# A planned two-layer trunk: copies exchanged for transfers, and the order planned anew with another account of the DMA engines

## The chip, the core and the metric

The kernel runs on one core of one Trainium2 chip. A core has five engines, each with its own in-order queue: TensorE (PE, with its weight loads as PEld), VectorE (DVE), ScalarE (ACT), GpSimd (POOL) and SyncE (SP), which here only issues transfers. An instruction waits on semaphores for what it needs, and everything behind it on its engine waits with it. The metric is the device time of one execution in microseconds, the median of several runs.

## The reference

Two layers are computed on x, 512 rows by 1024 columns, float32. Each layer is

```python
h = x @ w_in                          # 512x2048, cut into q, k, v, u (512 columns each)
A = diff_attention(q, k, v)           # 4 heads; rotary; two causal softmaxes, p0 - lam*p1; RMSNorm
B = s5_ssm(u)                         # 32 groups, complex diagonal scan over 512 steps; GELU; GLU
x = layer_norm(ALPHA*x + concat(A, B) @ w_out)
x = layer_norm(ALPHA*x + relu(x @ w_ff1)**2 @ w_ff2)      # inner width 4096
```

All of it has to hold to float32 accuracy. So each large product is made of three: both operands are split into a high part (a cast to the matmul type) and the remainder.

## The kernel before, in words

**Recording and planning.** The code in `trunk` doesn't issue instructions. It records them (`Rec.add`), with their tiles and dependences. `Rec.cost` gives each a duration, and for a transfer a time on the shared DMA engines (`op.move`) and a fixed part (`op.fix`). `Rec.run` then builds a list schedule by these numbers: each engine takes the ready instruction of the highest priority, which is the longest path behind it plus offsets from the table `PLAN` ("pri" by group of instructions, "fine" by single instruction, "ao", "so", "ap", "sp", "po" by kind). `issue` emits everything in the planned order. So an engine's order is decided by the table and the cost numbers together, before anything runs. Where the planner sees PE idle it may put products of a zero tile into the gap (`wz`, "fillers"); they do no useful work.

**Weights.** `wsplit` (and `gsplit` for the second feed-forward product) loads a block of 128 x 1024 into a `raw` buffer, casts it on ACT into `whi`, and makes the remainder `wlo` in one of three ways, chosen by letters in the table: "V" subtracts on DVE, "P" subtracts on POOL, "A" writes the negated block with ACT and lets POOL issue a DMA that adds the block in flight. There are five `raw` and four `whi`/`wlo` buffers. "lo" holds the letters of the input products, "flo" those of w_ff1, "glo" and "elo" those of w_ff2, "nlo" those of w_out. `mm3` makes the three matmuls of one product: high by high, and each high by the other's remainder.

**A layer.** The front part computes the blocks of "back" (u, q, k, v by number) on PE, and between them attention heads (`attn_u`, one per head and row block; `attn_fin` per head) and the four quarters of the S5 part (`ssm_pars` or `ssm_load`, `ssm_outp`, `ssm_a`, `ssm_b`, `ssm_c`). In layer 1 the first four blocks are multiplied by halves of the rows, since the rows of x come out of the layer norm before. Then come w_out with a layer norm, and eight steps of the feed-forward part, in which seven products replace eight ("m1" to "m7", with sums of weight blocks and of hidden blocks made on DVE), and the last step with the second layer norm.

**Copies and transfers.** Four places can move data within on-chip memory by ACT copies ("A") or by DMA ("D"), per layer: "um" rearranges u in `uproj` (D: one ACT copy into `rt`, a write to DRAM tile `ud`, four reads back), "qm" spreads q and k over partition halves in `qkproj` (D: one ACT cast and one DVE subtraction of the whole tile, then four transfers for q or eight for k; A: casts and subtractions by halves, and for k two memsets), and "mm" fills the block-Toeplitz matrix `mx` in `ssm_outp` (A: six ACT copies of 32 partitions and one of 128 per quarter; D: three transfers and the one copy). `start` loads the first two weight blocks and the eight slices of x in the order written, with "cuts" as the borders of the parts in which the weight blocks come.

**Names and lines.** In the trace all instructions that the planner issues stand at one line, L534, so tiles tell them apart: `whi`, `wlo` and `raw` are weights, `xTh` and `xTl` the split activations, `slot` and `xq` work tiles, `at` attention tiles, `mh` and `y` hold hidden activations of the feed-forward part and the halves of the mix, and `ps_acc`, `ps_sc` and `ps_s` the PSUM banks. "q1"-like names in the table are blocks. The planner's transfer times are at lines 296 to 298 and 485 to 487, `vproj` is at 1072, `attn_u` at 1110.

## Time and profile before

| | us |
|---|---|
| median of 3 runs (lowest, highest) | 1128.52 (1127.23, 1130.73) |
| profiled execution, its own time | 1130.64 |
| its span, first to last instruction | 1128.9 |
| PE busy | 1101.6 |
| DVE busy | 919.5 |
| ACT busy | 609.3 |
| POOL busy | 199.0 |

The profiled execution took 1130.64 us, of which 1.7 us lie outside the span. Times of single instructions are those of this execution. Matmul records overlap, as PE starts one before the other has left the array, so a stretch that is wholly busy can still be slowed by the clock or by small products. The column PEclk tells the granted clock: 1.00 is 2.4 GHz, 0.50 is 1.2 GHz.

### The profile page before, as it was taken

The page shows a single profiled execution, that of the slowest core. Times are in us where ns is not written, and L with a number is a line of the kernel's source. Part 1 is how long each engine was busy: PE and PEld are TensorE (multiplying, and loading weights), DVE is VectorE, ACT ScalarE, POOL GpSimd, SP SyncE. Part 2 cuts the span into 40 slices and gives each one's busy share as a digit, 9 for nine tenths or more (in the row PEclk, how much of TensorE's full clock was granted, in tenths as well). Part 3 has the DMA queues.
Part 4 walks back from the last instruction along what each step waited for, and adds up shares of the span by engine and source line. Part 5 has one row for each costly group of instructions (what it writes and reads, how often), then busy time and mean ns, then how long its engine had stood idle before and what let it go on. Part 6 is the DMA issues. An engine that isn't in the chain of part 4 may idle for free.

```text
span 1128.9 us, 15944 instructions
## 1 busy us (share of the span) xinstructions
PE 1101.6 (98%) x5738; PEld 929.7 (82%) x5738; DVE 919.5 (81%) x1575; ACT 609.3 (54%) x1060; POOL 199.0 (18%) x180
## 2 busy tenths in 40 slices
PE   9999989999999999999998999999999999999996
PEld 6889867898888888888788878888988888888885
DVE  7999998888778877877973789857778779778877
ACT  6557878246454464455343767952455445454440
POOL 1112111121211211211021221113112103103101
PEclk9999989999999999999999999999999999999999
DMA  9755645334555455465788764652444554565341
GB/s 312 193 138 109 161 124 155 116 112 115 147 159 131 122 164 134 119 178 148 224 226 208 179 163 106 194 145 81 141 131 131 149 149 119 144 159 148 105 130 74
DMA packets 59582, 167.73 MB, mean 149 GB/s; under 512 B 7408, under 2 KB 11888, under 8 KB 59504
## 3 DMA queue, kind: packets, MB, share of 16 engines
q1 hardware_dynamic: 48848, 127.92, 35.6%
q0 software_dynamic: 10656, 38.80, 18.6%
q8 instruction: 45, 0.74, 0.3%
q14 instruction: 33, 0.27, 0.1%
HBM read 112.17 MB, written 9.44 MB: 108 GB/s over the span
## 4 chain that ended last, share of the span: by engine, by line
PE 85%; DVE 6%; DMA 6%; ACT 3%; issue 1%; SPq 0%; POOL 0%; DVEq 0%; POOLq 0%; ACTq 0%
PE ps_acc L534 45%; PE ps_sc L534 28%; PE ps_s L534 12%; DVE slot L534 2%; DMA wlo<-raw 2%; DVE xq L534 1%; DMA rt<-rt 1%; DVE rt L534 1%; DMA raw<-in_w_v_dram 1%; DMA raw<-in_w_u_dram 1%; DMA keep<-xq 1%; DMA xq<-rt 1%; ACT at L534 0%; DMA slot<-in_xt_dram 0%; ACT whi L534 0%
## 5 line engine op out<-in xcount | busy, mean ns | idle before, releaser
L534 ACT CAST whi<-raw 128x1024 fp32r<-128x1024 f32 x222 | 233.3, 1051 | 284.2 <-PE ps_acc L534 177.9
L534 PE MATMUL ps_acc<-xTh,wlo 128*128 128x512 f32 (+1 forms) x712 | 268.5, 378 | 3.0 <-DMA wlo<-raw 1.9
L534 PE MATMUL ps_acc<-xTh,whi 128*128 128x512 f32 (+1 forms) x712 | 269.9, 380 | 0.7 <-ACT xTh L534 0.6
L534 PE MATMUL ps_acc<-xTl,whi 128*128 128x512 f32 (+1 forms) x712 | 268.7, 379 | 0.5 <-DVE xTl L534 0.5
L534 PE MATMUL ps_sc<-whi,slot 128*128 128x512 f32 x784 | 251.4, 390 | 1.3 <-DVE xq L534 1.3
L534 DVE TENSOR_TENSOR wlo<-raw,whi 128x1024 fp32r<-128x1024 f32 x114 | 139.0, 1226 | 56.6 <-ACT whi L534 56.6
L534 PEld LDWEIGHTS ps_sc<-whi,slot 128*128 128x128 f32 x784 | 147.1, 188 | 32.6 <-DVE xq L534 1.3
L534 POOL DMA_DIRECT2D wlo<-raw x74 | 65.0, 879 | 523.1 <-ACT rt L534 168.6
L534 PEld LDWEIGHTS ps_acc<-xTh,wlo 128*128 128x128 f32 x712 | 134.1, 188 | 26.7 <-DMA wlo<-raw 3.4
L534 PEld LDWEIGHTS ps_acc<-xTh,whi 128*128 128x128 f32 x712 | 134.0, 188 | 25.4 <-ACT xTh L534 1.8
L534 PEld LDWEIGHTS ps_acc<-xTl,whi 128*128 128x128 f32 x712 | 134.2, 188 | 24.2 <-DVE xTl L534 1.9
L534 PE MATMUL ps_sc<-wlo,slot 128*128 128x512 f32 x392 | 152.7, 390 | 0.0
L534 DVE TENSOR_TENSOR slot<-slot 128x512 fp32r<-128x512 f32 (+4 forms) x143 | 105.9, 755 | 7.8 <-ACT slot L534 7.0
L534 POOL TENSOR_TENSOR wlo<-raw,whi 128x1024 fp32r<-128x1024 f32 x34 | 85.0, 2501 | 151.5 <-ACT whi L534 124.2
L534 DVE TENSOR_TENSOR xq<-xq,ps_sc 128x512 f32<-128x512 f32 x124 | 83.6, 681 | 25.8 <-PE ps_sc L534 25.8
L534 ACT ACTIVATE wlo<-raw 128x1024 fp32r<-128x1024 f32 x74 | 78.3, 1060 | 29.0 <-PE ps_acc L534 18.5
L534 PEld LDWEIGHTS ps_sc<-wlo,slot 128*128 128x128 f32 x392 | 73.6, 188 | 15.2
L534 DVE TENSOR_TENSOR raw<-raw 128x1024 f32<-128x1024 f32 x56 | 68.2, 1218 | 14.2 <-DMA raw<-in_w_ff_dram 13.5
L534 ACT CAST slot<-slot 128x512 fp32r<-128x512 f32 x56 | 34.6, 618 | 50.9 <-DVE slot L534 48.4
L534 PE MATMUL ps_acc<-wlo,xTh 128*128 128x256 f32 (+1 forms) x176 | 55.6, 322 | 3.1 <-DMA wlo<-raw 3.1
L534 PE MATMUL ps_acc<-whi,xTh 128*128 128x256 f32 (+1 forms) x176 | 56.3, 324 | 0.2 <-ACT rt L534 0.2
L534 PE MATMUL ps_acc<-whi,xTl 128*128 128x256 f32 (+1 forms) x176 | 55.9, 321 | 0.0
(228 smaller groups left out, 1846.1 us busy)
## 6 DMA issues: line engine op xcount, KB each, us to landing
raw<-in_w_ff_dram SPq DMA_DIRECT2D x128, 512.0 KB, 3.6
wlo<-raw POOLq DMA_DIRECT2D x74, 512.0 KB, 5.3
raw<-in_w_qk_dram SPq DMA_DIRECT2D x16, 512.0 KB, 5.0
raw<-in_w_out_dram SPq DMA_DIRECT2D x16, 512.0 KB, 3.6
raw<-in_w_u_dram SPq DMA_DIRECT2D x8, 512.0 KB, 4.8
raw<-in_w_v_dram SPq DMA_DIRECT2D x8, 512.0 KB, 7.0
rt<-rt SPq DMA_DIRECT2D x64, 64.0 KB, 2.8
at<-in_ln_dram SPq DMA_DIRECT2D x16, 256.0 KB, 3.9
```

Source lines behind the costliest of these rows:

```text
L534: getattr(self.real[op.eng], op.name)(*[_real(x) for x in op.a], **{n: _real(x) for n, x in op.k.items()})
```

## The change

Four switches change sides. u of layer 1 goes from transfers to copies (u of layer 0 stays with transfers); q of layer 0 goes to copies and k of layer 0 to transfers; q of layer 1 goes to transfers; the Toeplitz blocks of both layers go to transfers. The first two weight blocks come in two parts of 256 and 768 columns. The first two row blocks of each head, not only the first, have both score maps in one bank, which takes one mask product and one maximum instead of two. The planner's account of a transfer is another: other rates and fixed parts, and a transfer that runs beside one of the other queue now slows that one too. The offsets ("pri", 130 groups; "fine"), the places of heads and S5 quarters, two lists of blocks and the letters of the remainders are all other ones. `vproj` has a second layout of its weights under the switch "vw", which is off in both layers.

```diff
-        "q0 u0 k0 u1 v0 u2 v1 q1 k1 u3 q2 v2 k2 v3 q3 k3 g0 g1 g2 g3".split(),
-        "u0 k0 u2 q0 u1 v0 v1 q1 k1 u3 v2 q2 k2 v3 q3 k3 g0 g1 g2 g3".split(),
+        "u0 q0 k0 u1 v0 u2 v1 q1 k1 u3 q2 v2 k2 v3 q3 k3 g0 g1 g2 g3".split(),
+        "u0 k0 u1 u2 q0 v0 v1 q1 k1 u3 v2 q2 k2 v3 q3 k3 g0 g1 g2 g3".split(),
     ],
-    "att": [[8, 11, 15, 19], [8, 12, 15, 18]],
-    "s5": [[1, 13], [10, 14]],
+    "att": [[8, 12, 14, 22], [9, 10, 15, 18]],
+    "s5": [[4, 14], [6, 14]],
...
-    "lo": ["AAAVAAPAAAAVAAAAAAAA", "AAAAAAAAAAAAAPAVAAVP"],
...
-    "flo": "VPVV",
-    "nlo": "APVAVPVA",
-    "glo": "APVVAAV",
+    "lo": ["AAAVPAPAAAAVAAAAAAAP", "AAAAAAAAAAAAAAAVAAVA"],
...
+    "flo": "AVPP",
+    "nlo": "APVAVPPV",
+    "glo": "AVPPAPV",
...
-    "elo": "VVVV",
+    "elo": "AVPV",
...
-    "cuts": [0, 8],
+    "cuts": [0, 2, 8],
...
-    "um": ["D", "D"],
-    "qm": ["DA", "AA"],
-    "mm": ["A", "A"],
+    "um": ["D", "A"],
+    "qm": ["AD", "DA"],
+    "mm": ["D", "D"],
...
-    "one": 1,
+    "one": 2,
...
-            op.move = rows * runs / 16 * (47.0 + o.idx.size * 4 / runs / 35.0) * (2.0 if e != "DMA" else 1.0)
-            op.fix = 50.0 if e != "DMA" or not on[0] else 990.0 if on[1] else 890.0
-            return (660.0 if rows < 128 else 500.0) if e == "DMA" else 1030.0, 1000.0 + op.fix + 1.3 * op.move
+            op.move = rows * runs / 16 * (33.0 + o.idx.size * 4 / runs / 32.1) * (1.7 if e != "DMA" else 1.0)
+            op.fix = 30.0 if e != "DMA" or not on[0] else 750.0 if on[1] else 586.0
+            return (660.0 if rows < 128 else 500.0) if e == "DMA" else 1030.0, 1463.0 + op.fix + 1.3 * op.move
...
-                q, z = ("POOL", "DMA") if e == "POOL" else ("DMA", "POOL")
-                b = max(move[q], op.t1 + 1000.0)
-                move[q] = b + op.move + min(op.move, max(0.0, move[z] - b))
+                q, z, r, u = ("POOL", "DMA", 0.515, 0.734) if e == "POOL" else ("DMA", "POOL", 0.266, 0.485)
+                b = max(move[q], op.t1 + 1463.0)
+                both = max(0.0, min(op.move / r, move[z] - b))
+                move[q] = b + op.move + both * (1 - r)
+                move[z] += both * u
```

How the order moves is seen at three places. The first is ACT near the end of layer 0's attention. Before, between a head's output (`jk`, `at<-ps_sc`) and the first exponentials of the next head (`at,smx<-ps_sc,nm`), ACT has this:

```order
L534 COPY at_1660<-ps_sc_1821 128x128
L534 CAST xq_1933<-rt_1783 64x512 x2
L534 ACTIVATE slot_1366<-slot_1366 128x512
L534 ACTIVATE at_1660<-at_1660,f4_1947 128x128 x4
L534 COPY mx0_108<-m3_1774 32x128 x3
L534 ACTIVATE mh_1974<-ps_sc_1954,sm_115 128x512
L534 COPY mx0_108<-m3_1774 32x128 x3
L534 COPY mx0_108<-m3_1774 128x128
L534 ACTIVATE y_1987<-ps_s5_1963 128x512
L534 ACTIVATE u_764<-ps_s5_1963 128x512
L534 CAST xq_1998<-rt_1783 64x512 x2
L534 ACTIVATE at_2011,smx_2012<-ps_sc_1907,nm_2003 128x128
```

Now, from the last Toeplitz copy of one quarter to the exponentials of the next head:

```order
L538 COPY mx0_98<-m3_1601 128x128
L538 ACTIVATE slot_1266<-slot_1266 128x512
L538 CAST xq_1753<-rt_1161 64x512
L538 CAST xq_1760<-rt_1161 64x512
L538 ACTIVATE y_1779<-ps_s5_1768 128x512
L538 ACTIVATE u_629<-ps_s5_1768 128x512
L538 ACTIVATE at_1822,smx_1823<-ps_sc_1790,nm_1814 128x128
L538 ACTIVATE at_1826,smx_1823<-ps_sc_1790,nm_1814 128x128
L538 COPY mx0_98<-m3_1642 128x128
```

The six 32-partition copies of `mx` have left ACT for SP's queue, and of the four half-tile casts of k two of q are left.

The second place is PE at the v blocks of layer 1: `ps_acc_6096` before and `ps_acc_6059` now are v0, `whi` and `wlo` its weights in two blocks. Before:

```order
L534 MATMUL ps_acc_6096<-whi_5988,xTh_141 128x256
L534 MATMUL ps_acc_6096<-wlo_6002,xTh_141 128x256
L534 MATMUL ps_acc_6096<-whi_5988,xTl_157 128x256
L534 MATMUL ps_acc_6096<-whi_6023,xTh_141 128x256
L534 MATMUL ps_acc_6096<-wlo_6012,xTh_141 128x256
L534 MATMUL ps_acc_6096<-whi_6023,xTl_157 128x256
L534 MATMUL ps_acc_6096<-whi_6023,xTh_141 128x256
```

Now, where `ps_acc_6091` is v1:

```order
L538 MATMUL ps_acc_6059<-whi_5952,xTh_131 128x256
L538 MATMUL ps_acc_6059<-wlo_5962,xTh_131 128x256
L538 MATMUL ps_acc_6059<-whi_5952,xTl_141 128x256
L538 MATMUL ps_acc_6059<-whi_5983,xTh_131 128x256
L538 MATMUL ps_acc_6059<-wlo_5972,xTh_131 128x256
L538 MATMUL ps_acc_6091<-whi_5952,xTh_131 128x256
L538 MATMUL ps_acc_6091<-wlo_5962,xTh_131 128x256
L538 MATMUL ps_acc_6091<-whi_5952,xTl_141 128x256
```

Before, v0 runs from the first weight block straight through the second. Now two products of the second block stand in v0, and PE goes on with v1 on the first block. The blocks ahead of v are u0, k0, u2, q0 and u1 before, and u0, k0, u1, u2 and q0 now.

The third is POOL in layer 0's feed-forward part, where `wlo<-raw` is the issue of an adding DMA and `wlo<-raw,whi` a subtraction on POOL. Before:

```order
L534 DMA wlo<-raw 128x1024 x3
L534 TENSOR_TENSOR wlo<-raw,whi 128x1024 x2
L534 DMA wlo<-raw 128x1024
L534 TENSOR_TENSOR wlo<-raw,whi 128x1024
L534 DMA wlo<-raw 128x1024 x2
L534 TENSOR_TENSOR wlo<-raw,whi 128x1024
L534 DMA wlo<-raw 128x1024 x3
L534 TENSOR_TENSOR wlo<-raw,whi 128x1024 x2
L534 DMA wlo<-raw 128x1024
L534 TENSOR_TENSOR wlo<-raw,whi 128x1024
```

Now:

```order
L538 DMA wlo<-raw 128x1024 x3
L538 TENSOR_TENSOR wlo<-raw,whi 128x1024 x2
L538 DMA wlo<-raw 128x1024
L538 TENSOR_TENSOR wlo<-raw,whi 128x1024 x2
L538 DMA wlo<-raw 128x1024
L538 TENSOR_TENSOR wlo<-raw,whi 128x1024 x5
L538 DMA wlo<-raw 128x1024
L538 TENSOR_TENSOR wlo<-raw,whi 128x1024
L538 DMA wlo<-raw 128x1024 x2
L538 TENSOR_TENSOR wlo<-raw,whi 128x1024
```

In each of the two feed-forward parts POOL has 38 such subtractions where it had 13, and DVE 22 where it had 48 and 47; the adding DMAs are 21 in both. Over the program the ACT copies into `mx` of 32 partitions go from 48 to none, the half-tile casts on ACT from 40 to 24, and 64 copies of 32 x 128 into `u` come to ACT in layer 1. SP issues 429 transfers instead of 391.

## Rows read from the trace of the kernel before

**Rows 1.** Page, part 1: engine, busy us, share of span, count.

```profile
PE 1101.6 (98%) x5738; PEld 929.7 (82%) x5738; DVE 919.5 (81%) x1575; ACT 609.3 (54%) x1060; POOL 199.0 (18%) x180
```

**Rows 2.** Stretches: length, each engine's busy us, PE clock, DMA share, GB/s.

```profile
0.00:10.00 10.00, 8.54 (x42) 5.40 (x43) 4.46 (x13) 5.70 (x8) 2.50 (x7) 1.00 0.83 279
...
147.00:151.50 4.50, 1.46 (x8) 0.76 (x8) 4.50 (x12) 3.38 (x10) 2.55 (x4) 1.00 0.87 222
...
151.50:161.70 10.20, 9.00 (x35) 7.49 (x36) 9.80 (x22) 8.24 (x24) 0.52 (x1) 0.50 0.24 83
...
205.00:530.00 325.00, 324.92 (x1552) 273.54 (x1551) 263.78 (x344) 158.10 (x209) 61.87 (x41) 1.00 0.48 132
...
530.00:611.00 81.00, 78.82 (x479) 69.71 (x478) 55.93 (x104) 35.40 (x54) 11.98 (x14) 1.00 0.79 220
...
615.70:619.10 3.40, 3.40 (x18) 3.40 (x18) 1.23 (x3) 0.00 (x0) 0.00 (x0) 0.50 1.04 287
...
619.10:745.00 125.90, 121.71 (x767) 104.29 (x767) 108.61 (x220) 101.08 (x243) 23.25 (x32) 1.00 0.60 157
...
745.00:1105.00 360.00, 359.85 (x1704) 301.89 (x1703) 277.01 (x355) 167.93 (x221) 64.77 (x43) 1.00 0.49 132
```

**Rows 3.** Timeline of PE near the start: start us, us, instruction, count.

```profile
5.92 0.50 PE L534 MATMUL ps_acc<-xTh,whi 128*128 128x512 f32 x1
...
24.49 2.36 PE L534 MATMUL ps_sc<-wz 128*128 128x256 bf16 x20
...
33.12 1.16 PE L534 MATMUL ps_sc<-wz 128*128 128x256 bf16 x9
```

**Rows 4.** Timeline of ACT at the end of layer 0's attention.

```profile
148.61 1.24 ACT L534 CAST xq<-rt 64x512 fp32r<-64x512 f32 x2 [0.68 <-DVE rt L534]
...
151.70 0.91 ACT L534 COPY mx<-m 32x128 f32<-32x128 f32 x3
...
153.35 1.22 ACT L534 COPY mx<-m 32x128 f32<-32x128 f32 x4
...
155.44 1.25 ACT L534 CAST xq<-rt 64x512 fp32r<-64x512 f32 x2
...
156.70 0.37 ACT L534 ACTIVATE at<-ps_sc,nm 128x128 f32<-128x128 f32 x1
```

**Rows 5.** Timeline of PE at the v products of layer 1.

```profile
614.47 0.39 PE L534 MATMUL ps_acc<-wlo,xTh 128*128 128x256 f32 x1 [3.10 <-DMA wlo<-raw]
```

**Rows 6.** The chain that ended last, same place: start us, us, what.

```profile
603.60 10.82 DMA wlo<-raw
```

**Rows 7.** DMA issues: tiles, queue, count, KB each, median us to landing.

```profile
wlo<-raw POOLq DMA_DIRECT2D x74, 512.0 KB, 5.3
...
rt<-rt SPq DMA_DIRECT2D x64, 64.0 KB, 2.8
...
xq<-rt SPq DMA_DIRECT2D x16, 128.0 KB, 5.7
...
u<-ud SPq DMA_DIRECT2D x32, 64.0 KB, 3.4
```

**Rows 8.** Groups by form: count, then busy us, mean ns, idle before.

```profile
L534 ACT CAST xq<-rt 64x512 fp32r<-64x512 f32 x40 | 24.7, 618 | 6.0 <-DVE rt L534 5.3
...
L534 ACT COPY mx<-m 32x128 f32<-32x128 f32 x48 | 14.2, 296 | 3.8 <-PE ps_s L534 3.0
...
L534 DVE TENSOR_TENSOR wlo<-raw,whi 128x1024 fp32r<-128x1024 f32 x114 | 139.0, 1226 | 56.6 <-ACT whi L534 56.6
...
L534 POOL TENSOR_TENSOR wlo<-raw,whi 128x1024 fp32r<-128x1024 f32 x34 | 85.0, 2501 | 151.5 <-ACT whi L534 124.2 <-PE ps_sc L534 27.3
...
L534 DVE TENSOR_TENSOR slot<-slot 128x512 fp32r<-128x512 f32 x56 | 54.4, 972 | 7.2 <-ACT slot L534 7.0
...
L534 DVE TENSOR_TENSOR slot<-mh,slot 128x512 fp32r<-128x512 f32 x32 | 34.3, 1096 | 0.0
```

**Rows 9.** One tile's instructions: duration ns smallest/median/largest, first and last start.

```profile
L534 DVE TENSOR_TENSOR slot<-mh,slot x32: 681/684/2882, 261.3 to 1098.2; 128x512 fp32r<-128x512 f32 x32
```

More of the change, by code (lines that the diff above doesn't have):

```diff
@@ L43 @@
     "back": [
[L44 to L48 removed]
+        "u0 q0 k0 u1 v0 u2 v1 q1 k1 u3 q2 v2 k2 v3 q3 k3 g0 g1 g2 g3".split(),
+        "u0 k0 u1 u2 q0 v0 v1 q1 k1 u3 v2 q2 k2 v3 q3 k3 g0 g1 g2 g3".split(),
+    ],
+    "att": [[8, 12, 14, 22], [9, 10, 15, 18]],
+    "s5": [[4, 14], [6, 14]],
     "bufs": {"slot": 13, "mh": 2, "y": 3, "xq": 13, "at": 4, "rt": 5, "u": 4},
     "ps": {"acc": 2, "sc": 4, "s5": 2},
[L51 to L55 removed]
+    "lo": ["AAAVPAPAAAAVAAAAAAAP", "AAAAAAAAAAAAAAAVAAVA"],
+    "eng": {"rope": ["VVV", "VVV"], "tab": ["VVVVVV", "VVVVVV"], "cg": ["VVVV", "VVVP"], "ch": ["VVVV", "PVVV"], "sa": ["PV", "PP"], "sb": ["VVVVVV", "VVVVVV"]},
+    "flo": "AVPP",
+    "nlo": "APVAVPPV",
+    "glo": "AVPPAPV",
     "seq": "f m1 m7 f m2 m4 f m6 f m5 m3",
[L57 removed]
+    "elo": "AVPV",
     "wb": 4,
[L59 removed]
+    "s5o": "p1 p0 o0 a0 b0 c0 o1 a1 p2 b1 a2 b2 p3 c1 a3 o2 b3 c2 o3 c3",
     "swq": "S",
[L61 to L64 removed]
+    "ao": [-6000, 34000],
+    "so": [2000, 7000],
+    "ap": [56500, 58750],
+    "sp": [37000, 45000],
     "pw": -6000,
@@ L73 @@
     "pt": "u",
[L74 removed]
+    "po": -18000,
     "m3": 4,
[L76 removed]
@@ L89 @@
+    "hv": 4,
+    "vw": [0, 0],
 }
@@ L1072, in vproj @@
     def vproj(l, z):
-        if z % 2 == 0:
-            v_w[l] = [w for c in range(2) for w in wsplit(w_v[l, z // 2, c], 1024, 4, lo_mode(l, f"v{z}") if l or z else "V")]
-        acc = bank(bt(l, f"v{z}"))
-        for b in range(2):
-            xb_ = xblk(2 * (z % 2) + b)
-            for k in range(KD):
-                mm3(acc[:, 256 * b:256 * b + 256], xb_[k], v_w[l][k], k == 0, k == KD - 1)
+        if PLAN["vw"][l]:
+            if z == 0:
+                v_w[l] = [w for c in range(4) for w in wsplit(w_v[l, c], 1024, 2, lo_mode(l, f"v{c}"))]
+            acc = bank(bt(l, f"v{z}"))
+            for k, x_ in enumerate(xblk(z)):
+                mm3(acc, x_, v_w[l][k], k == 0, k == KD - 1)
+        else:
+            if z % 2 == 0:
+                v_w[l] = [w for c in range(2) for w in wsplit(w_v[l, z + c], 1024, 4, lo_mode(l, f"v{z}") if l or z else "V")]
+            acc = bank(bt(l, f"v{z}"))
+            for b in range(2):
+                xb_ = xblk(2 * (z % 2) + b)
+                for k in range(KD):
+                    mm3(acc[:, 256 * b:256 * b + 256], xb_[k], v_w[l][k], k == 0, k == KD - 1)
         if z % 2 == 0:
@@ L1117, in vj @@
         def vj(j):
+            if PLAN["vw"][l]:
+                return v_t[l, j][:, h * P:(h + 1) * P]
             i = 256 * (j % 2) + 128 * (h % 2)
@@ L1399, in trunk @@
         else:
-            us = [z for z in PLAN["back"][l] if z[0] in "uqk"][:4]
-            for z, acc in zip(us, xprod([(z, t_) for z, t_ in zip(us, BANKS4)], l, HALVES)):
+            us = [z for z in PLAN["back"][l] if z[0] in "uqk"][:PLAN["hv"]]
+            for z, acc in zip(us, xprod([(z, t_) for z, t_ in zip(us, BANKS4)], l, HALVES) if us else []):
                 pre[l, z] = acc
@@ L1667, in _layout @@
     o["w_qk"] = w[:, :, :, 0:2].transpose(0, 4, 3, 2, 1, 5).reshape(L, 4, 2, 128, 1024)
-    o["w_v"] = (a["w_in"][:, :, 1024:1536].reshape(L, 2, 4, 128, 2, 256).transpose(0, 4, 1, 3, 2, 5)
-                .reshape(L, 2, 2, 128, 1024))
+    wv = a["w_in"][:, :, 1024:1536]
+    o["w_v"] = np.stack([wv[l].reshape(4, 2, 128, 512).transpose(0, 2, 1, 3).reshape(4, 128, 1024) if PLAN["vw"][l] else
+                         wv[l].reshape(2, 4, 128, 2, 256).transpose(3, 0, 2, 1, 4).reshape(4, 128, 1024) for l in range(L)])
     o["w_u"] = a["w_in"][:, :, 1536:].reshape(L, 8, 128, 4, 128).transpose(0, 3, 2, 1, 4).reshape(L, 4, 128, 1024)
```

11 lines of the change are left out of this document (2 added, 9 removed).

## The prediction

> **What bounds the kernel now.** I read the busy times first, then the span cut into stretches, then, for the stretches in which PE lost time, the timelines of PE and ACT and the chain of waits, and last the DMA issues and the groups by form. PE is busy for 1101.6 of 1128.9 us [rows 1], so 27.3 us are idle. The stretches tell where they are: the two feed-forward parts are 324.92 of 325 and 359.85 of 360 us busy [rows 2], so nothing can be won there, only lost. What is to be won lies in the two front parts, in five places.
>
> First the start: the first product of weights begins at 5.92 us [rows 3]. Second, 29 fillers run for 2.36 + 1.16 = 3.5 us between 24 and 35 us [rows 3], in which PE counts as busy and does nothing. Third, the end of layer 0's attention: PE works 1.46 of 4.50 us, then the granted clock stands at 0.50 (1.2 GHz) for 10.2 us, of which PE is busy 9.00 [rows 2]. At half clock 9.00 us of work give 4.50, so this place costs 3.04 + 1.20 + 4.50 = 8.7 us. The clock fell after the idle stretch, not before it. Fourth, the v products of layer 1: a wait of 3.10 us for the remainder of a weight block [rows 5], and behind it 3.40 busy us at half clock [rows 2], 1.7 us lost: 4.8 together. Fifth, the rest of layer 1's front: 81.00 - 78.82 = 2.2 and 125.90 - 121.71 = 4.2 us idle [rows 2], 6.4 together.
>
> What ends the third wait is ACT's queue. The next head's first exponential begins at 156.70, and since 148.61 ACT has had two half-tile casts of k, three and four copies into mx, and two casts more before it: 1.24 + 0.91 + 1.22 + 1.25 = 4.6 of 8.1 us [rows 4]. DVE is wholly busy in the first part of it and 9.80 of 10.20 us in the second [rows 2]. The fourth wait is a transfer: the adding DMA of the block takes 10.82 us [rows 6], where 5.3 is the median [rows 7], in a stretch with the DMA engines at 0.79 and more [rows 2].
>
> **The change part by part.** The sum is made against the profiled execution's own 1130.64 us; it stands 2.1 us above the median of 1128.52, so the result is carried over to the median by its difference.
>
> *Toeplitz blocks by transfers, q and k exchanged.* In layer 0 this takes 24 copies of 0.296 us from ACT, 7.1 us, and of the half-tile casts of 0.618 [rows 8] 16 of k go and 8 of q come, while one whole-tile cast per head moves from q to k and costs nothing: 4.9 us less. That is 12 us of ACT over layer 0. In the stretch of rows 4 six copies and, net, two casts go: 6 x 0.296 + 2 x 0.618 = 3.0 us before the exponential, close to the 3.04 that PE stood idle, and without the idle time the clock has no reason seen here to fall. So the place could give back the whole 8.7. Against it: the planner puts 24 fillers around there now where it put 12, at 2.36/20 = 0.12 us each [rows 3] 1.4 us more, and every head's k now ends in eight transfers, whose median is 5.7 us [rows 7] where the four casts took 2.5. I take -6.0 here. Bounds: -8.7 if nothing is late; below that nothing, since there is no more to win in this stretch. On the other side +2.0 for later k in the other three heads, with 0 to +8.7 as its ends (the same loss once more, at another head); 2.0 is nearer to the smaller end because a head's k is made many products before its scores.
>
> *The transfers' own price.* The 24 transfers into mx replace 48 copies and carry 16 to 48 KB; the nearest row is 64 KB in 2.8 us [rows 7], against 6 x 0.296 = 1.8 us of copies. They are needed only by the last products of a quarter, after its scan, which hides them; without that cover a quarter would be 1.0 us later, 8 us over eight quarters, the upper end. I take nothing.
>
> *First products in two parts.* Before the first product come 512 KB of weights and 256 KB of x, then 128 and 256. At the 279 GB/s of the first 10 us [rows 2] the 384 KB saved are 1.4 us, the most that can be won. The other end is +1.4 us, the same 384 KB missed later, since all of x and both blocks are needed before these products can finish. I take -0.8, near the middle of the gain, because SP has two transfers more to issue ahead of x.
>
> *Early fillers.* There are 16 where 29 were, 13 x 0.12 = -1.5 us. Ends: -3.5 (all 29 gone with what they covered) and +2.0 (the chain from the first q to the first scores, now with casts, is late again).
>
> *Layer 1: u by copies, other order.* The 256 KB write and the four reads per block of u go, which in this stretch means less for the weights' adding DMA to share. v's first use of its second remainder is still its fourteenth product, but v1 on the first block follows at once, which gives the other twelve products time. Of the 4.8 us I take half, -2.4, between -4.8 and +2.0. Against that ACT gets 64 copies; the nearest row, 32x128 from on-chip memory, has 0.296 us [rows 8], so 18.9 us, less 7.1 for mx and 4 x 0.618 = 2.5 for q: 9.3 us more on an engine that is busy 101.08 of 125.90 us there [rows 2]. That makes 110.4 of 125.9, still not the longest. In turn u no longer waits for a write and a read of 3.4 us [rows 7]; its sixteen copies take 4.7. Of the 6.4 us idle in the rest of this front I take -1.5; ends -6.4 and +18.9 (the second rival).
>
> *Remainders from DVE to POOL.* In the feed-forward parts POOL makes 50 more remainders at 2.50 us and DVE 51 fewer at 1.23 [rows 8]. Both engines have room for it: DVE works 263.78 of 325 us, POOL 61.87 [rows 2], and 25 x 2.50 is 62.5 more in each part. But a DVE instruction with two on-chip sources waits while POOL works on such an operand: the same subtraction takes 684 ns in the median and up to 2882 [rows 9], and the means of two of these groups are 1096 and 972 [rows 8], so 32 x 0.41 + 56 x 0.29 = 29 us were waited beside 34 POOL remainders, 0.9 us for each. By that 50 more cost DVE 43 us, and it saves 51 x 1.23 = 63. PE had no wait from those 29 us [rows 2]. So nothing for PE, between 0 and the third rival's price. The Trainium skill's page "SBUF — State Buffer", section "SBUF: two separate sides", says more: the pair of ports that the two engines share is held for a whole instruction and the other engine stands still. By it each added remainder could hold DVE for its full 2.5 us; the longest waits agree with that, the mean does not reach it, and the term would be the third rival's.
>
> *Smaller parts.* Eight fewer mask products and eight fewer maxima are below a filler's 0.12 us each on PE: -0.3, between -1.0 and 0.
>
> The sum: -6.0 + 2.0 - 0.8 - 1.5 - 2.4 - 1.5 - 0.3 = -10.5, so 1120.1 for an execution like the profiled one and 1128.5 - 10.5 = 1118.0 for the median.
>
> **The rivals.** *The losses move.* Every offset is another, so waits that go come back at other places, since the front parts have ACT and DVE near their limit anyhow: DVE had no free time in the stretch before the exponential [rows 2], and the changed order leaves that load nearly as it is. Then the seven terms cancel: about 1128.
>
> *ACT becomes the late engine in layer 1.* The place is the front of layer 1. Each u puts sixteen copies in a row on ACT, 4.7 us, and exponentials and weight casts stand behind them. If they are wholly on the path, 18.9 us come in place of the -2.4 and -1.5: 1128.5 - 6.6 + 18.9 = 1140.8. It ends slower as soon as more than 6.6 us plus the noise, some 10 of the 18.9, are on the path. For it: 80% busy already. Against it: the blocks of u come early there and their matrices late.
>
> *POOL holds DVE up in the feed-forward parts.* One wait of 2882 - 684 = 2.2 us that reaches PE in each of the fourteen planned steps would be 30.8 us: 1128.5 - 10.5 + 30.8 = 1148.8; it decides from five or six such steps. For it: five POOL remainders in a row now, 12.5 us, in which the hidden blocks' remainders stand on DVE. Against it: PE takes five blocks in more time than that, and DVE's load falls. The cited page's rule of the held ports speaks for this one.
>
> **How the numbers follow.** No change within 0.3%, 1125.1 to 1131.9, is what a measurement of this kernel can't tell apart. The forecast has 0.64, its own range 1110 to 1125 from its terms' ends (two thirds of the gains and of the new waits together); it is all faster. The losses moving have 0.19: 0.14 within, 0.05 above. ACT late has 0.10 and POOL late 0.07, both slower. So faster 0.64, same 0.14, slower 0.22. The range goes from 1109 to 1132; above it lie the two slower rivals, and little of the rest.
>
> **What would show it.** Right: no stretch at half clock between 120 and 200 us and the exponentials of the later heads not behind copies on ACT; the first product before 5.2 us; v's second block waited for less than 1.5 us; no low clock near 615; both feed-forward parts with less than 0.3 us of idle PE. Wrong: waits of PE for transfers of k in layer 0, for ACT after u's copies in layer 1, or for a DVE subtraction beside POOL in the feed-forward parts. If the idle time of PE is again above 25 us, the forecast is wrong whatever the places.

## The result, and the profile after

The changed kernel takes 1138.04 us (1136.64 to 1140.68, four runs) where the kernel before takes 1128.85 on the same chip: a ratio of 1.0085, with a 95% interval of 1.0064 to 1.0106. It is slower by 9.2 us. The forecast was 1118.0, its range ended at 1132. The profiled execution after has a span of 1135.3 us, 6.4 more than the one before. Of the 9.2 us, 0.9 more lie outside the span (2.6 us there after, 1.7 before), which no run explains, and 1.8 are there because the execution profiled before was that much slower than its median.

PE's busy time is 1.3 us less than before, so the loss is idle time. Part 1 of the page after answers to [rows 1]:

```profile
PE 1100.3 (97%) x5723; PEld 924.6 (81%) x5723; DVE 915.4 (81%) x1503; ACT 604.0 (53%) x1064; POOL 329.5 (29%) x234
```

The stretches after answer to [rows 2] and carry the same columns:

```profile
0.00:10.00 10.00, 7.30 (x32) 4.75 (x33) 3.85 (x14) 4.91 (x8) 2.51 (x7) 1.00 0.70 230
...
41.60:44.80 3.20, 0.04 (x1) 0.04 (x1) 3.20 (x13) 0.00 (x0) 0.00 (x0) 1.00 1.00 244
44.80:49.00 4.20, 4.05 (x20) 3.54 (x21) 4.17 (x18) 0.00 (x0) 0.00 (x0) 0.59 0.75 192
205.00:530.00 325.00, 320.71 (x1519) 269.07 (x1518) 257.29 (x316) 152.71 (x200) 112.36 (x63) 0.99 0.49 135
...
755.00:1115.00 360.00, 359.81 (x1707) 302.11 (x1707) 281.61 (x338) 168.35 (x221) 124.33 (x69) 1.00 0.50 133
```

Two places stand out: 3.2 us at 41.6 us in which PE stands and DVE is wholly busy, followed by a clock of 0.59, and a first feed-forward part that is no longer full (320.71 of 325). The second one is as full as before.

What PE waited for, the longest totals first (columns: us in total, times, longest us), after:

```profile
PE ps_sc L538 <- ACT at L538: 3.8, 5, 1.3
PE ps_acc L538 <- DVE wlo L538: 3.2, 1, 3.2
PE ps_sc L538 <- DVE xq L538: 3.0, 3, 2.3
PE ps_sc L538 <- DVE at L538: 2.5, 2, 2.0
PE ps_acc L538 <- ACT xTh L538: 2.3, 4, 0.8
PE ps_s L538 <- DVE slot L538: 1.6, 1, 1.6
```

and before:

```profile
PE ps_acc L534 <- DMA wlo<-raw: 5.0, 2, 3.1
PE ps_sc L534 <- ACT at L534: 3.0, 2, 2.5
PE ps_sc L534 <- DVE at L534: 1.7, 1, 1.7
```

The longest waits before were for an adding DMA, 5.0 us. Now 1.5 us of them are left. PE's waits for DVE have doubled, from 7.5 to 15.0 us over all tiles, and those for ACT went from 4.0 to 7.8.

To compare two orders that do not line up, I made a clock of useful work, called the ledger below: each matmul counts the median spacing to the next start that its shape has in the two traces, and fillers count nothing. Both programs have 1067 us of it. Time minus useful work is what was lost so far:

| useful us done | where | lost before | lost after | after minus before |
|---|---|---|---|---|
| 0 | first product | 5.7 | 5.0 | -0.7 |
| 20 | first blocks | 11.0 | 8.2 | -2.8 |
| 40 | v0, first scores | 14.0 | 16.1 | +2.1 |
| 80 | S5 quarter 0, q1 | 15.9 | 21.7 | +5.8 |
| 120 | before the end of attention | 17.8 | 23.3 | +5.5 |
| 140 | its worst stretch passed | 32.1 | 33.6 | +1.5 |
| 200 | layer norm | 33.2 | 37.4 | +4.2 |
| 340 | feed-forward, layer 0 | 33.2 | 38.9 | +5.8 |
| 360 | feed-forward, layer 0 | 33.2 | 43.1 | +9.9 |
| 560 | layer 1, ahead of v | 37.3 | 48.2 | +11.0 |
| 580 | layer 1, v0 done | 42.3 | 48.4 | +6.1 |
| 1060 | end | 52.1 | 58.9 | +6.8 |

So the gains that were forecast at the start, at the end of attention and at layer 1's v did come: 0.7, 4.0 and 4.9 us, and 2.1 between the first product and 20 us. Against them stand 4.9 us around v0, 3.7 up to quarter 0, 2.7 behind the attention, 1.6 and 4.1 in the first feed-forward part. These are single executions, but the other traces of the two orders, from the experiments below, agree: up to 120 us of useful work six executions of the old order lost 18 to 20.5 us and eight of the changed one 23 to 26. Between 120 and 200 us the old order lost 14.2 to 15.5 and the changed one 14.1 to 16.0, so over this longer stretch the gain of 4.0 at the end of attention is gone again.

### The profile page after: what moved, and what is told of

Same layout as the page of the kernel before. It is cut to its first block, busy times and chain, and to the rows that moved or that the text cites. A ratio compares the mean times of both kernels' runs of the same rounds, so it can differ in the third digit from the quotient of the medians.

```text
span 1135.3 us, 15967 instructions
## 1 busy us (share of the span) xinstructions
PE 1100.3 (97%) x5723; PEld 924.6 (81%) x5723; DVE 915.4 (81%) x1503; ACT 604.0 (53%) x1064; POOL 329.5 (29%) x234
## 4 chain that ended last, share of the span: by engine, by line
PE 77%; DMA 8%; DVE 7%; ACT 3%; issue 3%; SPq 1%; DVEq 0%; POOL 0%; ACTq 0%; POOLq 0%
PE ps_acc L538 40%; PE ps_sc L538 27%; PE ps_s L538 10%; DVE xq L538 2%; DMA rt<-rt 2%; DMA wlo<-raw 2%; DMA xq<-rt 1%; DMA raw<-in_w_qk_dram 1%; DVE rt L538 1%; DVE slot L538 1%; SPq L538 1%; ACT whi L538 1%; DMA raw<-in_w_u_dram 1%; ACT at L538 1%; DMA slot<-in_xt_dram 1%
## 5 line engine op out<-in xcount | busy, mean ns | idle before, releaser
L538 ACT CAST whi<-raw 128x1024 fp32r<-128x1024 f32 (+1 forms) x224 | 232.9, 1044 | 245.7 <-PE ps_acc L538 105.9
L538 POOL TENSOR_TENSOR wlo<-raw,whi 128x1024 fp32r<-128x1024 f32 x82 | 207.2, 2531 | 299.8 <-ACT whi L538 296.1
L538 DVE TENSOR_TENSOR slot<-slot 128x512 fp32r<-128x512 f32 (+4 forms) x139 | 127.4, 934 | 10.8 <-ACT slot L538 10.3
L538 DVE TENSOR_TENSOR raw<-raw 128x1024 f32<-128x1024 f32 x56 | 84.2, 1503 | 18.0 <-DMA raw<-in_w_ff_dram 11.3
L538 DVE TENSOR_TENSOR wlo<-raw,whi 128x1024 fp32r<-128x1024 f32 (+2 forms) x66 | 78.3, 1188 | 14.1 <-ACT whi L538 13.5
```

The lines of the kernel that those rows point to most:

```text
L538: getattr(self.real[op.eng], op.name)(*[_real(x) for x in op.a], **{n: _real(x) for n, x in op.k.items()})
```

## The experiments

Each kernel keeps the planned order of the kernel it is made from, and only the named instructions are moved or exchanged after planning, unless it is said that the order is planned anew. So no other instruction changes its place. Ratios are to the kernel before, measured on the same chip; the runs were spread over several chips, so two edited kernels are compared by their ratios where these come from different chips. The diffs are shortened to what the edit does.

**An earlier remainder for v0.** The DVE remainder that ended the 3.2 us wait moves ahead of S5's table work:

```diff
+ by["0v0.5"].t0 = 36520.0    # planned time in ns; the DVE subtraction of v0's second block
```

> The changed kernel in its own planned order, with one instruction moved: the DVE subtraction that makes the second remainder of layer 0's first v block goes ahead of some 25 small S5 table instructions on DVE, about 4 us earlier. Theory 1 (two single places cost the change its gain): the 3.17 us wait of PE at 41.6 us and the 3.4 us at half clock behind it go, 4.9 us in all, and nothing else is late: 1138.0 - 4.9 = 1133.1, with a span near 1130.5. Rival (DVE is the bound of this stretch, so PE's saved time comes back as a wait a little further on): between 1136.5 and 1138.

It took 1140.31 us, 1.0094 of before (1.0076 to 1.0112): nothing won. The timeline of PE in that run shows why:

```profile
46.34 1.09 PE L542 MATMUL ps_sc<-xq 128*128 128x256 f32 x3 [4.08 <-DMA xq<-rt]
```

The remainder is in time, and PE stands 4.08 us at the same place for the transfers of layer 0's first k. In the changed kernel these were late as well, the eight of them flying from 37.3 to 47.9 us, hidden behind the remainder. The rival holds in its result, though not in its reason: the next limit there is a transfer.

**Fillers in that wait.**

```diff
+ for i in range(28): order.append(c)    # c: product of the zero tile, c.t0 = by["0v0.19"].t0 - 1.0
```

> The changed kernel in its own planned order, with 28 fillers of 0.11 us (products of the zero tile, 3.1 us) put in front of the v product that waits 3.17 us at 41.6 us. Theory 2 (from the ends of that wait in the earlier runs: DVE is full from 15 to 57 us and can't deliver sooner; the fillers that the change dropped there had filled the same wait and kept the clock up): the wait is filled, no half clock at 44 to 53 us, 1.7 to 3.4 us are won, 1134.6 to 1136.3. If the clock has nothing to do with the wait, or the fillers come on top of it: 1138 to 1141.

It took 1140.31 us, 1.0095 (1.0072 to 1.0118). The stretch from 41.5 to 49 us, first in the changed kernel, then with the fillers:

```profile
41.50:49.00 7.50, 4.18 (x21) 3.59 (x21) 7.47 (x30) 0.00 (x0) 0.00 (x0) 0.77 0.86 214
```

```profile
41.50:49.00 7.50, 6.18 (x49) 5.02 (x48) 7.46 (x29) 0.00 (x0) 0.00 (x0) 1.00 0.77 195
```

The clock stayed at 1.00, as expected, and up to 40 us of useful work only 0.6 us less was lost (15.4 instead of 16.1). Two waits of 0.6 us for `xq<-rt` follow at once. So the slow clock cost little here. Executions of this order differ by more than 0.6 us at that point (15.5 to 19.5 us lost), so a small price can't be told from none; the theory's 1.7 to 3.4 us did not come. That PE would have stood still anyway is what the two waits suggest.

**No early fillers in the kernel before.**

```diff
+ order = [o for o in order if hasattr(o, "key") or not 20e3 < o.t0 < 36e3]   # 29 fillers out
```

> The kernel before in its own planned order, without the 29 fillers between 24 and 35 us. Theory 2: PE comes 3.3 us earlier to products whose operands DVE makes, waits 2.5 to 4 us more there and the clock falls for 3.4 to 6.8 us: 0 to +3.5 us, 1128.7 to 1132. If the fillers are idle work, as my prediction had it: -1.5 to -3.3, 1125.4 to 1127.2.

It took 1130.62 us, 1.0015 of before (1.0000 to 1.0030). PE's timeline there, with the fillers and without:

```profile
27.08 0.38 PE L534 MATMUL ps_acc<-whi,xTh 128*128 128x256 f32 x1 [0.24 <-ACT rt L534]
```

```profile
28.21 0.38 PE L538 MATMUL ps_acc<-whi,xTh 128*128 128x256 f32 x1 [2.44 <-ACT rt L538]
```

The wait ahead of this product was 0.24 us with the fillers and is 2.44 without them, nearly the time of the 20 fillers [rows 3]; where the other nine stood, a wait of 0.76 us appears. They covered waits. Removing them wins nothing; whether it loses 1.7 us or none, the interval leaves open.

**Rotation later.** In the changed order DVE stands at 77 us for a rotation's transfers, which take 5.8 us beside two adding DMAs:

```profile
76.36 0.67 DVE L538 TENSOR_TENSOR slot<-ct,api 128x512 f32<-128x512 f32 x1
79.56 1.29 DVE L538 TENSOR_TENSOR rt<-rt,rot 128x512 f32<-128x512 f32 x2 [2.53 <-DMA rt<-rt]
```

Behind it stands the instruction that PE waits 1.55 us for. The edit puts the three rotary instructions behind it:

```diff
+ for i, k in enumerate(("0q1.34", "0q1.33", "0q1.35")): by[k].t0 = by["0q1.37"].t0 - 9.0 + i
```

> The changed kernel in its own planned order, with the three rotary instructions of layer 0's q of head 1 placed 3 us later on DVE, behind a remainder and the last instruction of S5 quarter 0 that PE waits for. In every run of this order so far DVE stood 2.3 to 3.8 us at 77 to 81 us for the transfers of that rotation, which fly beside two adding DMAs, and PE then 1.2 to 1.7 us. Theory 3 (DVE sets the pace of layer 0's front, and this is where the change lost most of it): DVE's idle time there falls below 1 us, PE's wait goes, 1.5 to 2.9 us less: 1135 to 1136.5. Rival (another instruction is late right behind): within 1 us of 1138.

It took 1140.69 us, 1.0107 (1.0089 to 1.0125). DVE's idle time there fell from 2.5 to three pieces, 1.5 us together:

```profile
79.81 1.23 DVE L543 TENSOR_TENSOR wlo<-raw,whi 128x1024 fp32r<-128x1024 f32 x1 [0.33 <-ACT whi L543]
81.34 0.69 DVE L543 TENSOR_TENSOR rt<-rt,rot 128x512 f32<-128x512 f32 x1 [0.31 <-DMA rt<-rt]
82.87 0.69 DVE L543 TENSOR_TENSOR rt<-rt,rot 128x512 f32<-128x512 f32 x1 [0.83 <-ACT xq L543]
```

PE's wait went, and between 60 and 80 us of useful work 2.1 us were lost instead of 3.0. The total shows nothing of it: a wait of 0.86 us comes at 88.5, and more is lost by 120. Nothing is won, as the rival had it.

**All of POOL's remainders on DVE**, in both feed-forward parts:

```diff
+ if o.eng == "POOL" and o.name == "tensor_tensor" and o.tiles[0].key[1] == "wlo" and (235e3 < o.t0 < 530e3 or 775e3 < o.t0 < 1085e3): o.eng = "DVE"
```

> The changed kernel in its own planned order, with the 76 remainders that POOL subtracts in the two feed-forward parts subtracted on DVE, at the same places in the order. Theory 1: the wait of 2.27 us at 382.9 us and the half clock behind it (4.15 us together) come from POOL's 2.5 us per remainder, which frees the raw buffer late, so that its next load runs into an adding DMA; it goes, 1138.0 - 4.1 = 1133.9. Rival (the loss is a meeting of S5 table work, a load and an adding DMA that this order makes whatever engine subtracts): within 1 us of 1138. Second rival (DVE gets 76 x 1.2 = 91 us and becomes late): 1140 to 1150.

It took 1136.87 us, 1.0062 (1.0044 to 1.0080). The loss inside the part is settled by the traces: 6.0 us between 200 and 500 us of useful work in the changed kernel (6.4 in the runs with the early remainder and with the later rotation), 2.4 here. In the changed kernel PE stood for DVE, which stood for a transfer:

```profile
383.25 1.22 DVE L538 TENSOR_TENSOR raw<-raw 128x1024 f32<-128x1024 f32 x1 [5.51 <-ACT rt L538]
```

```profile
385.21 0.47 PE L538 MATMUL ps_sc<-whi,slot 128*128 128x512 f32 x1 [2.27 <-DVE xq L538]
```

The ACT instruction that DVE's row names had been done for 0.9 us. What came last is an adding DMA, issued at 375.75, whose source buffer the sum is written into; it landed at 383.1, after 7.3 us:

```profile
wlo<-raw POOLq DMA_DIRECT2D x1, 512.0 KB, 7.3
```

It shared the DMA engines with a load issued at 375.28, as soon as a POOL remainder (372.82 to 375.26) had freed that load's buffer. With the remainders on DVE the load went 1.4 us ahead of the adding DMA instead of 0.5, the adding DMA took 5.7 us, and PE waited 0.52:

```profile
387.77 0.47 PE L544 MATMUL ps_sc<-whi,slot 128*128 128x512 f32 x1 [0.52 <-DVE xq L544]
```

What POOL costs DVE shows in the groups by form, first in the changed kernel, then with the remainders on DVE (mean ns behind the busy us):

```profile
L538 DVE TENSOR_TENSOR raw<-raw 128x1024 f32<-128x1024 f32 x56 | 84.2, 1503 | 18.0 <-DMA raw<-in_w_ff_dram 11.3 <-ACT rt L538 5.5 <-DMA wlo<-raw 0.8
...
L538 DVE TENSOR_TENSOR wlo<-raw,whi 128x1024 fp32r<-128x1024 f32 x62 | 75.6, 1220 | 10.5 <-ACT whi L538 9.9
...
L538 DVE TENSOR_TENSOR slot<-slot 128x512 fp32r<-128x512 f32 x56 | 74.1, 1328 | 10.5 <-ACT slot L538 10.3 <-PE ps_sc L538 0.2
L538 DVE TENSOR_TENSOR slot<-mh,slot 128x512 fp32r<-128x512 f32 x32 | 34.1, 1081 | 0.4 <-ACT slot L538 0.4
...
L538 DVE TENSOR_TENSOR slot<-y 128x512 f32<-128x512 f32 x14 | 17.4, 1246 | 0.1
```

```profile
L544 DVE TENSOR_TENSOR wlo<-raw,whi 128x1024 fp32r<-128x1024 f32 x137 | 167.1, 1221 | 79.2 <-ACT whi L544 78.0 <-issue 1.1
...
L544 DVE TENSOR_TENSOR raw<-raw 128x1024 f32<-128x1024 f32 x56 | 68.3, 1219 | 10.2 <-DMA raw<-in_w_ff_dram 5.2 <-ACT whi L544 4.8
L544 DVE TENSOR_TENSOR slot<-slot 128x512 fp32r<-128x512 f32 x56 | 38.4, 685 | 9.2 <-ACT slot L544 9.2
L544 DVE TENSOR_TENSOR slot<-mh,slot 128x512 fp32r<-128x512 f32 x32 | 21.7, 684 | 0.0
...
L544 DVE TENSOR_TENSOR slot<-y 128x512 f32<-128x512 f32 x14 | 9.6, 685 | 0.1
```

15.9 + 35.7 + 12.4 + 7.8 = 71.8 us less in the four groups shown, and 7.1, 5.1, 3.8, 2.3 and 2.1 in five smaller ones (`slot<-y,slot`, `slot<-slot,mh`, `slot<-slot,y`, `u<-bbt`, `u<-bss,stc`): 92.2 us for 76 remainders, 1.21 us each. The subtractions themselves cost DVE 167.1 - 75.6 = 91.5 us. So giving these remainders to POOL relieves DVE of nothing. DVE's total on the page is even 10 us lower with all of them on DVE:

```profile
PE 1100.6 (97%) x5723; PEld 925.2 (81%) x5723; DVE 905.2 (80%) x1578; ACT 603.6 (53%) x1064; POOL 140.0 (12%) x159
```

What reached PE is 3.6 us, at one place, by way of a buffer that POOL freed late. Why the whole run won 1.2 us in the median and not 3.6: its profiled execution had lost 4.4 us more than the changed kernel's before the part began, in instructions that are the same in both. The runs with the early remainder allow a cleaner comparison, on one chip.

**Both edits together.**

> Both edits together: the early v remainder and all feed-forward remainders of POOL on DVE. Theory 1: 1138.0 - 4.9 - 4.1 = 1129.0, the time of the kernel before. Rivals as for the two alone: about 1137 if neither place is what it seems.

1136.11 us, 1.0054 (1.0035 to 1.0074). Against the early remainder alone, on the same chip, that is 4.2 us less for the remainders on DVE: the 3.6 us of the feed-forward part and some 0.5 outside the span. Theory 1, that two single places cost the gain, falls; the feed-forward half of it stands.

**Three places mended**: later rotation, remainders on DVE, and one adding DMA of the first feed-forward step turned into a DVE subtraction.

> The changed kernel in its own planned order with three places mended: the rotation of q of head 1 later (as in the run beside this), the feed-forward remainders of POOL on DVE, and the second w_ff1 block of layer 0 subtracted on DVE in place of an adding DMA that PE waits 0.8 to 2.7 us for. Theory 3: 1138 - 2 (rotation) - 3.6 (what the ledger showed for the remainders) - 1.3 = 1131. Rival (losses come back elsewhere): 1134 to 1137.

1137.23 us, 1.0069 (1.0051 to 1.0088): the rival. Between 200 and 500 us only 1.1 us are lost, 1.3 less than with the remainders on DVE alone, but up to 200 us 8.7 more are lost than before, and a wait of 2.0 us for layer 1's v0 is there again.

**Toeplitz blocks by copies in the changed order**, and **by transfers in the order before**:

```diff
- Q.dma_start(out=mx[0:(t + 1) * 32, t], in_=m3[(3 - t) * 32:128])
+ for r in range(t + 1): A.copy(mx[r * 32:(r + 1) * 32, t], m3[(r + 3 - t) * 32:(r + 4 - t) * 32])   # and the reverse
```

> The changed kernel in its own planned order, with the 24 transfers into the Toeplitz blocks replaced by the 48 copies of 32 partitions on ACT, at the places of the transfers. If the transfers are what gave back 4 us at the end of layer 0's attention (6 copies of 0.3 us taken from before the exponentials there), the loss at 147 to 162 us grows by 2 to 6 us, with a half clock again: 1140 to 1144. If the new order gave it back and not the transfers: 1137 to 1139. If the transfers cost something (Toeplitz blocks late behind SP's queue): below 1137.

> The kernel before in its own planned order, with the 48 copies of 32 partitions into the Toeplitz blocks replaced by 24 transfers on SP's queue, each where the first copy of its block stood. If ACT's copies are what made layer 0's attention end late (the run with copies in the changed order lost 6.4 us by them): the idle time at 148 to 151 us shrinks by 1 to 3 us and the 10.2 us at half clock by half or all, -3 to -8: 1120.7 to 1125.7. If other work of ACT and DVE is late there as well: -1 to 0.

With copies the changed kernel takes 1144.45 us (1.0134, 1.0110 to 1.0157), some 6 more. At the end of attention 6.8 us at half clock come back, and 1.4 us more are lost between 120 and 140 us of useful work. With transfers the kernel before takes 1126.68 (0.9988, 0.9973 to 1.0004), so its time alone doesn't show a gain. At the end of layer 0's attention, where I expected it, the second changes next to nothing; PE still waits 2.48 us for ACT:

```profile
151.52 1.06 PE L542 MATMUL ps_sc<-cs,at 128*128 128x128 f32 x3 [2.48 <-ACT at L542]
```

The 10.2 us at half clock stand too:

```profile
152.00:162.00 10.00, 9.11 (x38) 7.52 (x38) 9.86 (x23) 6.53 (x19) 0.66 (x2) 0.52 0.29 95
```

What the trace shows as won lies in layer 1. The stretch from 618 to 745 us, before and with transfers:

```profile
618.00:745.00 127.00, 122.81 (x772) 105.39 (x772) 108.61 (x220) 101.08 (x243) 23.25 (x32) 1.00 0.61 158
```

```profile
618.00:745.00 127.00, 126.16 (x792) 108.73 (x792) 110.77 (x225) 97.75 (x231) 23.25 (x32) 1.00 0.61 161
```

4.2 us of idle time become 0.8. Between 580 and 700 us of useful work 5.6 us are lost instead of 9.5, and in the changed order the copies lose 13.7 instead of 10.3. By these pairs of traces the transfers are worth 3.4 to 3.9 us in layer 1, in both orders.

**Layer 1's v0 remainder on DVE, in the kernel before.**

```diff
- A.activation(lo, raw, AF.Copy, scale=-1.0); G.dma_start(out=lo, in_=raw, accum_op=ALU.add)
+ V.tensor_tensor(lo, raw, hi, op=ALU.subtract)      # second block of 1v0 alone
```

> The kernel before in its own planned order, with the second remainder of layer 1's first v block subtracted on DVE (idle there from 590 to 602 us) in place of the negation on ACT and the adding DMA that took 10.82 us. Theory: the wait of 3.10 us at 611.4 and the 3.4 us at half clock behind it go, 4.8 us: 1123.9. Rival (the next transfer-fed operand is late instead, since the DMA engines are full there): -1 to -2.5, 1126.2 to 1127.7.

1125.80 us, 0.9968 (0.9954 to 0.9982): 3.6 us by the ratio, 2.0 to 5.2 by its interval, which lies between theory and rival. The trace settles it. The stretch from 600 to 625 us, before and with the edit:

```profile
600.00:625.00 25.00, 21.90 (x143) 20.22 (x142) 15.09 (x27) 12.79 (x18) 4.51 (x6) 0.93 0.76 189
```

```profile
600.00:625.00 25.00, 24.23 (x167) 21.60 (x166) 17.84 (x31) 13.29 (x18) 4.99 (x7) 1.00 0.76 200
```

Between 560 and 580 us of useful work 0.3 us are lost instead of 5.0. Nothing came in its place up to 700 us.

**Both of these.**

> The kernel before in its own planned order, with the Toeplitz blocks by transfers and the second remainder of layer 1's first v block on DVE. If the two gains add (3.6 us in layer 1 by the transfers, 4.6 us by the remainder, as their traces show them): 1128.7 - 8.2 = 1120.5. If they share a part: 1122 to 1124.

1123.38 us, 0.9961 (0.9946 to 0.9975): faster than both kernels, by 4.8 us than the one before and by some 14 than the changed one. In time it can't be told from the remainder alone (0.9968), so that the transfers add to it rests on the trace. The traces show the two gains nearly whole in layer 1 (10.8 us lost between 500 and 700 instead of 18.1); 2.8 us more were lost before 40 us, where nothing was edited.

**And a head's norm earlier.** Three small instructions of a head's norm at the end of layer 0's attention go ahead of a rotation:

> The same as the run beside it, and three small instructions of a head's norm at the end of layer 0's attention (two on DVE, one on POOL) placed ahead of a rotation, since PE waited 2.48 us at 148.4 for the scaling behind them. If that wait is what starts the 10.2 us at half clock: 0.8 us of waiting and 2 to 5 us of slow clock go, 1115 to 1118. If DVE sets the pace of that stretch whatever the clock: 0 to -0.8, 1119.7 to 1120.5.

1124.74 us, 0.9966 (0.9952 to 0.9979), no better. PE's wait for ACT there was 2.67 us, and 10.24 us at half clock came again. So this did not shorten the wait, and what would is open. How little the clock itself costs there shows in the six traces of the old order: with 10.2 us at half clock there, 13.6 to 14.5 us were lost between 120 and 140 us of useful work, and with 6.8 us, in the runs without the fillers, with the remainder and with both edits, 13.1 to 14.2. DVE was busy 9.80 of the 10.20 us [rows 2].

**The parts of the change that had no term**: the account of transfers alone, the changed kernel without it, and the four switches alone, each planned anew.

> The kernel before with only the new account of transfers (rates, fixed parts, and transfers of the two queues slowing each other); its table of offsets and all switches as before. Theory 4 (a table of offsets fits only the account that it was found with, whatever account that is): slower than before by 4 to 15 us, 1133 to 1143, with new waits all over the two front parts. Rival (the new account by itself makes a better order, and it is the new table or the switches that lose): 1122 to 1128.

> The changed kernel with the old account of transfers in its planner, all else as changed. Theory 4: slower than the changed kernel by 4 to 15 us, 1142 to 1153. Rival (the new account is what costs layer 0's front its 6 us and the first feed-forward part its 4): 1128 to 1134.

> The kernel before with the four switches alone (u of layer 1 by copies, q of layer 0 by copies and k by transfers, q of layer 1 by transfers, Toeplitz blocks by transfers), planned anew with the old table and account. Theory 4: the table doesn't fit these instructions, slower than before by 4 to 15 us, 1133 to 1143. Rival (the switches are worth what layer 1's front gained, some 3 to 8 us, and need no new table): 1120 to 1126.

1153.75 us (1.0215, 1.0188 to 1.0242), 1159.67 (1.0271, 1.0250 to 1.0292) and 1166.62 (1.0329, 1.0306 to 1.0353). The direction of theory 4 holds, with larger prices than its 4 to 15 us. In these three runs the table of offsets fits only the account and the switches that stand with it, and exchanging one of them alone costs 22 to 38 us. Which of the new parts, each with a table of its own, would win or lose, they don't show.

**k of layer 0 by casts in the changed order**, alone and with the earlier remainder. What both leave out: the whole-tile cast goes, but DVE's whole-tile subtraction of k stays, on a tile that the cast no longer fills and ahead of the copies that read its result. So they compute another k, and DVE has 0.7 us more per head than their texts say.

```diff
- 8 transfers into the four xq tiles
+ four half-tile copies on ACT, two half-tile subtractions on DVE, two memsets on POOL
```

> The changed kernel in its own planned order, with the eight transfers of each k of layer 0 turned back into casts and subtractions by halves (four copies on ACT, two subtractions on DVE, two memsets on POOL, at the places of the transfers; the whole-tile cast and subtraction go). Theory 5 (at 41 to 48 us two things are late at once, the v remainder on DVE and k's transfers, which take from 37.3 to 47.9 us; each hides the other): with the transfers alone gone the wait for the remainder stays, the further waits for xq (0.9 to 3.6 us) go: 1136 to 1138. Rival (DVE's load is all that counts there, and two subtractions by halves cost it 0.7 us per head more than one): 1139 to 1141.

> The same, and the second v remainder moved ahead as in the earlier run. Theory 5: both limits of that place are gone, so the 4.1 us of waiting and the slow clock behind it go: 1138.5 - 5 = 1133 to 1134.5. Rival (DVE): 1138 to 1140, and the first scores wait for a DVE instruction instead.

1149.13 us (1.0171, 1.0147 to 1.0195) and 1149.23 (1.0168, 1.0143 to 1.0193), 11 us more than with the transfers. With both edits the wait at 41.5 us is 1.2 us, and one of 5.0 us for ACT's copy of v follows at 49.7. ACT had stood for DVE ahead of it, for a row maximum behind the table work:

```profile
52.35 0.37 ACT L559 ACTIVATE at<-ps_sc,nm 128x128 f32<-128x128 f32 x1 [9.45 <-DVE nm L559]
```

A late DVE instruction is what the rival had, though at another place and with a smaller loss. The casts stand here in an order that was planned for transfers, with the extra subtraction in front of them, so these two runs don't settle what the transfers of k cost. They lend theory 5 no support.

## Why the prediction was wrong, step by step

*The failed steps.* The step that failed is the sum's count of new waits. It had six gains and one new wait, "+2.0 for later k in the other three heads". The gains I could name came to 11.7 us in the ledger. The new losses came to 17.0 where I had 2.0. PE is idle for 1135.3 - 1100.3 = 35 us, above the 25 that were to refute the forecast. They are mostly not where the kernel before lost time. They are where it lost little or nothing: layer 0's front ahead of the end of attention, of which I had read only the start and the fillers, and the first feed-forward part, whose rows I had read as safe.

*Early fillers, -1.5.* The first failure by place. I took them for idle work. They stood in front of a wait, and the run without them shows that PE then waits as long. The change had 26 fillers fewer by 40 us of useful work. It was 2.8 us ahead at 20 us, and had lost 2.1 more at 40. The end that I had given, "+2.0 (the chain from the first q to the first scores, now with casts, is late again)", is nearest to what happened, though by other links than the casts: DVE is full there (rows of 41.6 and 44.8 us), a remainder of v on it was late, and the transfers of k stood late behind it.

*Later k, +2.0.* Between 40 and 120 us of useful work the change lost 3.4 us more, and 2.7 more behind 140. The trace names DVE behind a rotation for the larger single piece; waits for transfers into `xq` were 0.9 us in the profiled execution, up to 6.1 in others. Three edits that each took one of these waits away, or filled it, left the total where it was, and a different wait came each time. What bounds this front is thus not one late instruction. That DVE, ACT and the transfers are all near their limit in it is my reading, not shown by a run that relieves all of them.

*Toeplitz blocks and k, -6.0 at the end of attention.* The place gave back 4.0, and 1.3 if one counts to 200 us of useful work. The sign that I had named came true: no half clock is left there. The stretch from 120 to 200 us of useful work, before and after:

```profile
138.00:233.50 95.50, 89.97 (x475) 73.32 (x475) 86.83 (x177) 61.87 (x149) 18.47 (x18) 0.95 0.44 127
```

```profile
143.30:237.40 94.10, 88.11 (x480) 70.65 (x480) 82.49 (x170) 57.16 (x136) 23.15 (x19) 1.00 0.49 141
```

PE's idle time rose from 5.5 to 6.0 us, in more and shorter waits for ACT and DVE. I had priced the half clock at 4.50 us, as if PE could use a faster clock while DVE was busy 9.80 of 10.20 us; the traces with 6.8 us of it lost hardly less than those with 10.2. The cause of the wait was wrong too. I read "what ends the third wait is ACT's queue" from copies that stand before the exponential at 156.70. The wait of 2.48 us ended at 150.85, before the first of these copies. The wait, and the rows that ended it, ACT and POOL of the kernel before:

```profile
150.85 0.33 PE L534 MATMUL ps_sc<-cs,at 128*128 128x128 f32 x1 [2.48 <-ACT at L534]
```

```profile
150.41 0.97 ACT L534 ACTIVATE at<-at,f 128x128 f32<-128x128 f32 x3
```

```profile
148.81 1.04 POOL L534 TENSOR_TENSOR f<-f,mhalf 128x4 f32<-128x4 f32 x1 [3.50 <-DVE f L534]
```

ACT's scaling waited for a head's norm, which went DVE, POOL, DVE. The transfers in the old order left the place as it was, and copies in the new order lost 1.4 us of the 4.0, so most of it came with the new order. The transfers were worth 3.4 to 3.9 us in layer 1, where I had counted them only as less load on ACT. Of their own price, taken as nothing, the trace after shows no wait, the old order with transfers one of 0.89 us.

*Remainders, 0 for PE.* A POOL remainder held DVE for 1.21 us where I had 0.9, because I counted two groups of instructions and more of them wait. So DVE's load did not fall by 63 - 43 = 20 us: over the two feed-forward stretches it went from 540.8 to 538.9. That none of it reaches PE was wrong by 3.6 us, and 1.3 us more in that part came from an adding DMA that the letters put in the first step. The third rival had PE wait for DVE instructions that POOL holds up. What came is another path: POOL freed a buffer late, the load into it met an adding DMA, and DVE waited for that, in one step of fourteen. The second feed-forward part lost nothing, with as many remainders on POOL.

*Layer 1's v, -2.4.* The late remainder was the right cause, and the size was halved without a reason: the ledger has 4.9, and the edit of this alone 4.7. Which of the two reasons given, v1 in between or fewer transfers beside it, made it come in time is not shown; in one of eight executions of the changed order the wait was there with 2.0 us.

*Start, -0.8.* Right in size: the first product began 0.73 us sooner, at 5.19. No run has this edit alone.

*Rest of layer 1, -1.5, and copies of u.* +0.6 between 580 and 700, although the Toeplitz transfers gave 3.4 there. So the new order lost some 4 us of its own in this front too; its longest waits there are for DVE, 1.95 and 1.24 us. The second rival, 18.9 us by copies of u, did not come.

*The rivals.* "The losses move" is what happened, and it was priced at 1128 with a chance of 0.19, as if moved losses could at worst cancel the gains. It has no such floor: a new order can lose more than the old one won. With the order changed in every stretch, the range should have reached further up for it.

## What to carry to other kernels

Where a change re-plans an order, a sum over the old trace's idle places counts only what can be won. Here most of the new waits fell in stretches that were nearly full, so read there which engine is busy all the time and what the new order puts ahead of the instructions that feed the bound engine. Before a stretch at half clock is priced at half of PE's busy time, look whether another engine is full in it. Before a copy is blamed for a wait, check that it stands before the end of that wait. And a single late operand in a tuned order, moved to an idle engine with everything else kept, gave here what a new plan with many changes did not.

## What the runs showed of the hardware

Fillers in front of waits cost nothing here: with 29 of them out of the program the time was 1.0015 of before (1.0000 to 1.0030), and the wait behind the first 20 was 2.2 us longer. PE at half clock cost little where DVE was full: three executions with 6.8 us of it at the end of attention lost 13.1 to 14.2 us there, three with 10.2 us lost 13.6 to 14.5. A subtraction of 128x1024 on POOL, 2.5 us long, held DVE up for 1.21 us on average over 76 of them, which is what the same subtraction takes on DVE (1.22). Instructions with two on-chip sources waited, but also a copy with one (`u<-bbt`, 765 ns in the mean beside them and 212 without). A 512 KB load that was issued 0.5 us ahead of an adding DMA took 7.2 us, and the adding DMA 7.3; the load just before, alone on the engines for most of its time, took 3.4.
